# One select per attention item, with differences of two blocks' values, in a hybrid decoder block

## The chip, the cores and the metric

One core of a Trainium2 chip runs one decoder block on 2048 tokens. The metric is the device time of one execution in microseconds (us), the median of several runs. The engines are TensorE (PE, matmuls; PEld is its weight load), VectorE (DVE), ScalarE (ACT), GpSimd (POOL) and SyncE (SP, which issues the transfers). Each engine works through its own instructions in order and waits for the others by semaphores.

## The reference

The residual stream has 2048 tokens of 1024 numbers. What matters here is the first half of the block, cut to its core:

```python
h = rmsnorm(x, attn_norm)
z = h @ w_in            # -> [pool channels | q | k | v | gate_pool | gate_attn]
gates = sigmoid(z[gate part] + b_gate)
a = pool_mixer(u_pool, w_pool, pool_scale)      # causal means over 2, 4, 8, 16 tokens
q = partial_rope(rmsnorm(q, q_norm), positions) * scale
k = partial_rope(rmsnorm(k, k_norm), positions)
b = swa_sink_attention(q, k, v, sinks)          # 16 query heads, 2 key heads of 64
x = x + (g_pool * a + g_attn * b) @ w_out
# then rmsnorm, up-projection, causal convolution of 3, SiLU gate, down-projection
```

A query sees itself and the 127 tokens before it: in blocks of 128, the keys of its own block up to its own place, and the keys of the block before from the place after that. So each key place of 128 belongs to one of two blocks, and which one depends on whether it lies at or before the query's place.

## The kernel before, in words

The tokens are taken in two chunks (c = 0, 1) of 1024 tokens, or 8 blocks. All large matmuls are three products of high and low parts (`mm3`, L225 before and L235 after; the same weight tile, 8 steps of 3, makes a "fill" of 24 matmuls of 128x512). The parts are made by an ACT copy and a DVE subtraction (L209 and L210 for weights).

At the start, the head, the pool weights are folded (`fold`) while the first tokens and weights arrive; the tables of sines and cosines (`rope_tables`, L501 to L537) are made on DVE by one long chain of small operations. Then, in each chunk, a first stage makes keys and values block by block, with some fills between. Then comes attention: 32 items, in 4 groups of 4 heads (`q4` = 3, 2, 1, 0), each over 8 blocks. An item is

- scores: 8 matmuls into the one PSUM bank `s` (L770),
- on DVE: L779 copies the scores of the block before over the places that this query doesn't see in its own block (both blocks then share 128 key places), L784 takes the maximum, L785 and L786 scale and bound it; four exponentials on ACT (L791), and the normalisation (L795),
- transposes on PE into bank `t` (L802), the copy into high and low parts (ACT L804, DVE L805) as tile `M`,
- two selects on POOL (L808, L811), which separate the places of the own block from those of the block before,
- values: 4 matmuls into bank `a` (L824), copied out by L831 and L832 into `ob`, and multiplied with the gate by L834.

Between the items stand one or two fills each: projections of the attention gates (`ga`), the pool gates (`pg`), the pool channels (`pu`) and the queries (`q`). `fillers` and `first_fillers` deal them out to the places; `slabs_of(i)` are the two column slabs that belong to group i. Queries go to DRAM as high and low parts (`qd`) and come back item by item (`load_queries`), two items ahead. Small work behind a fill is collected in `later` and issued by `run_later`; the window sums of the pool channels are `windows` (L874, L885 and L886). The weights' order in SP's queue is `weight_order`: in the second chunk they are read back as ready parts (`made_...`). A scheduler with its own model of times then sets each engine's final order, so the code's order is only a wish. Tiles named `U`, `F`, `M`, `Q` and `R` are buffers of pools of 19, 4, 5, 5 and 3.

Of the kernel before, what the change touches and what calls it, by code (L numbers as in the profile page):

```python
# [121 lines left out]

def fillers(c, i):

    ga = [[("ga", ct, n) for n in range(2)] for ct in slabs_of(i + 1) if i < 3]
    pg = [[("pg", ct, n) for n in range(2)] for ct in slabs_of(i - 1) if i > 0]
    pu = [[("pu", ct, n) for n in range(2)] for ct in slabs_of(i)]
    fold = [[("fold", j, 0)] for j in FOLDS[FOLD_FIRST:] if c == 0 and i == 0]
    q = [queries_of(i)] if i < 2 else []
    out = sum(ga[:1] + pg[:1] + q + fold + pu[:1] + ga[1:] + pg[1:] + pu[1:], [])  # L130
    return [out[n * len(out) // NB:(n + 1) * len(out) // NB] for n in range(NB)]


def first_fillers(c):

    ga = [("ga", ct, n) for ct in slabs_of(0) for n in range(2)]
    q = queries_of(2) + queries_of(3)
    if c > 0:
        return [q[0:1], q[1:2], q[2:3], q[3:4], q[4:5], q[5:6], q[6:7], q[7:8] + ga]
    fold = [("fold", j, 0) for j in FOLDS[FOLD_LEAD:FOLD_FIRST]]  # L140
    return [[], fold[0:1], fold[1:2] + q[0:2], fold[2:3] + fold[3:4], q[2:4], q[4:5], q[5:6],
            q[6:8] + ga]


def weight_order():
    out = []
    for c in range(NCH):
        if c > 0:
            out.append(("kv",))
        else:  # L150
            out += [("fold", j) for j in FOLDS[:FOLD_LEAD]]
        out += [(kind, j) for parts in first_fillers(c) for kind, j, n in parts if n == 0]
        for i in range(4):
            out += [(kind, j) for parts in fillers(c, i) for kind, j, h in parts if h == 0]
        out += [("pg", ct) for ct in slabs_of(3)]
# [27 lines left out]
def block_kernel(ctx: ExitStack, tc: tile.TileContext, x, xT, pos, vec, qkn, w_poolT, w_pool, w_q, w_kv,  # L183
# [12 lines left out]
    qp = pool("qp", 5)  # L196
# [8 lines left out]
    def split(hi, lo, src):  # L205
        n = src.shape[1] // 2
        for i in range(2):
            t = slice(i * n, (i + 1) * n)
            A.copy(hi[:, t], src[:, t])  # L209
            V.tensor_sub(lo[:, t], src[:, t], hi[:, t].bitcast(F32))  # L210
# [49 lines left out]
    def split_weights(key, raws):  # L260
# [10 lines left out]
        for raw in raws:  # L271
            shape = [P, 2] + list(raw.shape)[1:]
            p, tag = (mp, "M") if out and key[1] not in FOLDS[:FOLD_LEAD] else (up_, "U")
            out.append(p.tile(shape, F32R, tag))
            hi, lo = out[-1][:, 0], out[-1][:, 1]
            split(hi, lo, raw)
# [84 lines left out]

    one = cp.tile([P, 1], F32, "one")
# [65 lines left out]
    for i in range(2):  # L428
# [4 lines left out]
    ones = qp.tile([P, P], F32, "Q")  # L433
    V.memset(ones, 1.0)
    identr = cp.tile([P, P], F32R, "identr")
    G.affine_select(identr, ones, pattern=[[-1, P]], base=0, channel_multiplier=1,
                    compare_op=ALU.is_equal, fill=0.0)
# [11 lines left out]
    hbg = cp.tile([P, 16], F32, "hbg")  # L449
    nsink = cp.tile([P, NH], F32, "nsink")  # L450
# [5 lines left out]
    def scaled():  # L456
        V.tensor_scalar(hbg, vc[:, V_BG:V_BG + 16], 0.5, None, op0=ALU.mult)
        V.tensor_scalar(nsink, vc[:, V_SK:V_SK + NH], -1.0, None, op0=ALU.mult)
# [6 lines left out]
    fix = cp.tile([P, 4, 16], F32, "fix")  # L465
    V.memset(fix, 1.0)
    for g, w in enumerate(WINDOWS):
        for t in range(w - 1):
            V.memset(fix[:, g, t:t + 1], w / (t + 1.0))
# [4 lines left out]
    kc = cp.tile([P, 2, 2, P], F32R, "kc")  # L474
    vcar = cp.tile([P, 2, P], F32R, "vcar")
# [20 lines left out]
    def rope_tables(chunk):  # L496

        n, at = [P, NB, 8], slice(chunk * NB, (chunk + 1) * NB)
        rt = mp.tile([P, 12, NB, 8], F32, "M")
# [126 lines left out]
    def rope(dst, src, b, nh):  # L626

        t = sp.tile([P, 2, nh, 16], F32, "rope", 1)
# [20 lines left out]
    def keys_values(c, hs, ws):  # L649
        kts = [up_.tile([P, 2, T], F32R, "U") for _ in range(2)]  # L650
        vs = up_.tile([P, NB, 2, P], F32R, "U")
# [10 lines left out]
        def block_a(n, pk):  # L662
# [3 lines left out]
            A.activation(vs[:, n, :, 0:HD], pv, AF.Copy, scale=rn)  # L666
            V.scalar_tensor_tensor(vs[:, n, :, HD:P], pv, rn, vs[:, n, :, 0:HD].bitcast(F32),
                                   op0=ALU.mult, op1=ALU.subtract)
            r = head_rstd(pk, 2, c, n)
            kq = kns[n] = qp.tile([P, 2, 80], F32, "Q")  # L670
            kn = kq[:, :, 0:HD]
            V.tensor_tensor(kn, pk[:, 0:128].rearrange("p (g d) -> p g d", g=2),
# [3 lines left out]
        def block_b(n):  # L676
            c_, kq = slice(n * P, (n + 1) * P), kns.pop(n)
            kn, kr = kq[:, :, 0:HD], kq[:, :, HD:80]
            rope(kr, kn, c * NB + n, 2)
# [15 lines left out]
        return kts, vs, raw, block_a, block_b, turn  # L695
# [9 lines left out]
    def queries(c, j, n, hs, ta, st):  # L705
        if n == 0:
            st["q", j] = stream.get("q", j, later=later)
        pq, c_ = project(hs, st["q", j], n, "fa"[j % 2])
        sq = qp.tile([P, 512], F32, "Q")
        A.square(sq, pq)  # L710
        if j % 2 == 0:
            st["even"] = pq, sq
            return
        pe, acc = st.pop("even")
# [4 lines left out]
        for i, src in ((at - 1, pe), (at, pq)):  # L719
            t = mp.tile([P, 2, 512], F32R, "M")  # L720
            A.copy(t[:, 0], src)
            V.tensor_sub(t[:, 1], src, t[:, 0].bitcast(F32))
            for e, r in enumerate(STARTS[i]):
                load(qd[own][n][:, r:r + 8].rearrange("a d h t -> (d h) a t"),
                     t[64 * e:64 * e + 64].bitcast(F32))
# [12 lines left out]
    def rotate(a, b, rows, c_):  # L738
# [3 lines left out]
        ga, gb = (vc[h, V_QG + i:V_QG + i + 1] for i in range(2))  # L742
        t = mp.tile([P, 2, 512], F32, "M")
        for i, (x, g) in enumerate(((a, ga), (b, gb))):
            V.scalar_tensor_tensor(t[h, i], x[h], g, s, op0=ALU.mult, op1=ALU.mult)
            V.scalar_tensor_tensor(x[h], x[h], g, c, op0=ALU.mult, op1=ALU.mult)
        V.tensor_sub(a[h], a[h], t[h, 1])
        V.tensor_add(b[h], b[h], t[h, 0])

    def load_queries(it):  # L750
# [5 lines left out]
        it["rq"] = rq[:, q4 // 2, n, h:h + 4]  # L756

    def scores(it):
# [6 lines left out]
        for h in range(4):  # L765
# [7 lines left out]
            if n == 0 and b > 0:  # L773
                for a in range(2):
                    nc.tensor.matmul(sc[:, h, 0:P], st, kc[:, g, a, :], start=(a == 0),
# [22 lines left out]
    def probabilities(it):  # L798
        b = it["c"] * NB + it["n"]
        pp = ps.tile([P, 4, P], F32, "t")  # L800
        for h in range(4):
# [4 lines left out]
        pin = pa.bitcast(F32).rearrange("p a h q -> p (a h) q")  # L806
        cur = mp.tile([P, 2, 4, P], F32R, "M")
        G.affine_select(cur.rearrange("p a h q -> p (a h) q"), pin, pattern=[[0, 8], [1, P]],  # L808
                        base=0, channel_multiplier=-1, compare_op=ALU.is_ge, fill=0.0)
        if b > 0:  # L810
            G.affine_select(pa.rearrange("p a h q -> p (a h) q"), pin, pattern=[[0, 8], [-1, P]],  # L811
                            base=0, channel_multiplier=1, compare_op=ALU.is_gt, fill=0.0)
        it.update(cur=cur, prev=pa)

    def values(it):
        c, n, g, vs = it["c"], it["n"], it["q4"] // 2, it["vs"]
        todo = [(vs[:, n, g, :], it["cur"])]
        if c * NB + n > 0:
            todo.append((vs[:, n - 1, g, :] if n > 0 else vcar[:, g, :], it["prev"]))
# [8 lines left out]
        pe = pv.rearrange("p (c e) q -> p e c q", e=2)  # L828
        for e in range(2):
# [4 lines left out]
        V.scalar_tensor_tensor(tt, tt, 1.0, ob, op0=ALU.add, op1=ALU.mult)  # L834
# [12 lines left out]
    def gate_attn(c, ct, n, hs, ta, st):  # L847
        if n == 0:
            st["ga", ct] = stream.get("ga", ct, later=later)
            if ct % 2 == 0:  # L850
                ta[ct // 2] = up_.tile([P, 2, T], F32, "U")
        pg, c_ = project(hs, st["ga", ct], n)
        V.tensor_mul(pg, pg, rB[:, c_])
        A.activation(ta[ct // 2][:, ct % 2, c_], pg, AF.Tanh, scale=0.5, bias=hbg[:, 8 + ct:9 + ct])
# [12 lines left out]
    def windows(c, ct, u, st):  # L867
        g, win = ct // 2, WINDOWS[ct // 2]
# [14 lines left out]
        def finish():  # L883
            if c == 0:
                V.tensor_mul(s[:, 16:32], s[:, 16:32], fix[:, g, :])  # L885
# [460 lines left out]
    def mixer(c, hs, kvw):  # L1346
# [38 lines left out]
        for i in range(len(items)):  # L1385
            group, n = divmod(i, NB)
            scores(items[i])
            if i + 2 < len(items):
                load_queries(items[i + 2])
            fills = fillers(c, group)[n]  # L1390
            if i > 0 and len(fills) == 1:
                probabilities(items[i - 1])
            run_later()
# [7 lines left out]
        for n in range(2):  # L1401
            gated(c, slabs_of(3)[0], n, hs, ta, st)
        values(items[-1])
        run_later(9)
        if c + 1 < NCH:
            for g in range(2):
                A.copy(kc[:, g], kts[g][:, :, T - P:T].bitcast(F32))
            A.copy(vcar, vs[:, NB - 1].bitcast(F32))
        ms = [mixed(ta, j) for j in (3, 2, 1)]
        for n in range(2):  # L1410
            gated(c, slabs_of(3)[1], n, hs, ta, st)
# [3 lines left out]
    scaled()  # L1415
# [86 lines left out]
```

## Time and profile before

| | us |
|---|---|
| runs | 2477.36, 2484.81, 2481.82 (median 2481.82) |
| profiled execution | 2475.48, span 2473.8 |
| PE busy | 2416.9 (98%) |
| DVE busy | 1901.9 (77%) |
| ACT busy | 1101.3 (45%) |
| POOL busy | 226.5 (9%) |
| L808, 64 selects | 84.7, 1323 ns each |

The profile comes from one execution; its own time is 2475.48 us. In rows of the trace "x24" is a count, "a<-M,U" names what is written and read, and a bracket at the end says how long the engine stood idle before and who released it. The attention of the first chunk lies at about 142 to 530 us, that of the second at 1356 to 1745 us.

### The profile page before, as it was taken

How to read it: one execution, taken by the hardware profiler on the slowest of the kernel's cores; microseconds unless marked ns; L12 is line 12 of the kernel's file. 1: busy time of each engine (PE TensorE's matmuls, PEld its weight loads, DVE VectorE, ACT ScalarE, POOL GpSimd, SP SyncE). 2: the span in 40 equal slices, each digit the busy share in tenths (PEclk: the TensorE clock that was granted, in tenths of full speed). 3: DMA queues.
4: the chain of work that ended last, by engine and by line, in shares of the span. 5: the costliest groups of instructions: out<-in, count | busy, mean ns of one | idle time of the engine just before them, and what ended most of it. 6: DMA issues, size and time to landing. Idle time of an engine off the chain costs nothing.

```text
span 2473.8 us, 30606 instructions
## 1 busy us (share of the span) xinstructions
PE 2416.9 (98%) x11360; PEld 2003.3 (81%) x11360; DVE 1901.9 (77%) x3047; ACT 1101.3 (45%) x2106; POOL 226.5 (9%) x161
## 2 busy tenths in 40 slices
PE   7999999899999999999999999999999999999999
PEld 6887887777888888888888888777888888887887
DVE  7668778977887887899844666678569888788994
ACT  6443444445455555543512333334435555454432
POOL 0112322310000000000002113213000000000000
PEclk9999999999999999999999999999999999999999
DMA  9662725248332233544343432320553222228321
GB/s 338 231 214 84 243 98 177 75 167 275 128 103 77 85 115 116 179 179 162 109 163 120 137 128 86 141 94 22 168 190 102 78 78 93 86 68 281 127 78 51
DMA packets 137620, 336.68 MB, mean 136 GB/s; under 512 B 12160, under 2 KB 47232, under 8 KB 126464
## 3 DMA queue, kind: packets, MB, share of 16 engines
q1 hardware_dynamic: 137472, 334.74, 39.7%
q8 instruction: 89, 1.46, 0.2%
q14 instruction: 59, 0.48, 0.1%
HBM read 230.88 MB, written 103.81 MB: 135 GB/s over the span
## 4 chain that ended last, share of the span: by engine, by line
PE 80%; DVE 12%; ACT 3%; DMA 2%; issue 2%; POOL 1%; SPq 0%; DVEq 0%; ACTq 0%; POOLq 0%
PE f L225 22%; PE f L1037 18%; PE t L1037 9%; PE a L225 4%; PE a L1037 4%; PE a L1327 4%; PE f L1327 4%; PE s L1327 4%; PE t L1327 4%; PE s L770 1%; ACT Q L791 1%; DVE F L874 1%; DVE U L210 1%; PE a L824 1%; DVE Q L832 1%
## 5 line engine op out<-in xcount | busy, mean ns | idle before, releaser
L225 PE MATMUL f<-U,U 128*128 128x512 f32 (+1 forms) x3552 | 832.6, 390 | 16.3 <-DVE U L210 7.6
L225 PEld LDWEIGHTS f<-U,U 128*128 128x128 f32 x3552 | 654.6, 189 | 151.0 <-DVE U L210 11.4
L1037 PE MATMUL f<-U,U 128*128 128x512 f32 x1512 | 359.7, 389 | 1.3 <-ACT Q L1055 1.3
L1037 PEld LDWEIGHTS f<-U,U 128*128 128x128 f32 x1512 | 283.3, 188 | 61.5 <-ACT Q L1055 2.2
L1103 DVE SCALAR_TENSOR_TENSOR M<-F,vc,M 128x1024 f32<-128x1024 f32 x176 | 224.9, 1281 | 128.2 <-ACT M L1100 127.8
L1037 PE MATMUL t<-U,U 128*128 128x512 f32 x1080 | 254.2, 389 | 0.0
L1037 PEld LDWEIGHTS t<-U,U 128*128 128x128 f32 x1080 | 202.7, 188 | 42.1
L791 ACT ACTIVATE Q<-s,st,rq 128x128 f32<-128x128 f32 x256 | 114.2, 452 | 157.9 <-DVE st L786 145.6
L321 ACT CAST U<-R 128x1024 fp32r<-128x1024 f32 x120 | 125.5, 1053 | 65.6 <-DVE R L342 33.9
L322 DVE TENSOR_TENSOR U<-R,U 128x1024 fp32r<-128x1024 f32 x120 | 146.6, 1221 | 0.1
L225 PE MATMUL a<-U,U 128*128 128x256 f32 (+1 forms) x768 | 142.3, 339 | 2.1 <-DVE M L510 1.3
L1037 PE MATMUL a<-U,U 128*128 128x512 f32 x576 | 138.6, 389 | 0.0
L808 POOL TENSOR_SCALAR_AFFINE_SELECT M<-M 128x1024 fp32r<-128x1024 f32 x64 | 84.7, 1323 | 569.7 <-DVE M L805 391.6
L225 PEld LDWEIGHTS a<-U,U 128*128 128x128 f32 x768 | 119.5, 189 | 17.7 <-ACT rB L570 1.5
L1037 PE MATMUL f<-U,M 128*128 128x512 f32 x504 | 122.3, 390 | 4.1 <-DVE F L1081 4.1
L1037 PEld LDWEIGHTS a<-U,U 128*128 128x128 f32 x576 | 108.0, 188 | 22.3
L1286 ACT CAST U<-U 128x1024 fp32r<-128x1024 f32 x74 | 77.0, 1050 | 86.9 <-PE a L1327 26.9
L1037 PEld LDWEIGHTS f<-U,M 128*128 128x128 f32 x504 | 94.4, 188 | 24.4 <-DVE F L1081 4.9
L210 DVE TENSOR_TENSOR U<-R,U 128x512 fp32r<-128x512 f32 x142 | 97.8, 721 | 17.3 <-ACT U L209 17.2
L1100 ACT ACTIVATE M<-F,vc 128x1024 f32<-128x1024 f32 x88 | 109.2, 1243 | 1.3
L1089 ACT COPY F<-f 128x512 f32<-128x512 f32 x42 | 24.6, 586 | 178.7 <-PE f L1037 178.7
L1287 DVE TENSOR_TENSOR U<-U,U 128x1024 fp32r<-128x1024 f32 x74 | 89.5, 1218 | 10.6 <-ACT U L1286 10.6
(270 smaller groups left out, 3754.2 us busy)
## 6 DMA issues: line engine op xcount, KB each, us to landing
R<-w_up SPq DMA_DIRECT2D x80, 512.0 KB, 3.7
actd<-M SPq DMA_DIRECT2D x44, 512.0 KB, 2.6
U<-w_down SPq DMA_DIRECT2D x88, 256.0 KB, 5.2
U<-actd SPq DMA_DIRECT2D x88, 256.0 KB, 5.3
qd<-M SPq DMA_DIRECT2D x64, 256.0 KB, 3.4
Q<-qd SPq DMA_DIRECT2D x64, 256.0 KB, 3.0
R<-w_out SPq DMA_DIRECT2D x32, 512.0 KB, 5.1
U<-kept SPq DMA_DIRECT2D x12, 1024.0 KB, 6.5
```

The costliest lines, as they stand in the source:

```text
L210: V.tensor_sub(lo[:, t], src[:, t], hi[:, t].bitcast(F32))
L225: nc.tensor.matmul(out, a, b, start=(i == 0), stop=(i == n - 1))
L321: A.copy(t[:, 0], raw)
L322: V.tensor_sub(t[:, 1], raw, t[:, 0].bitcast(F32))
L791: A.activation(pr[:, h, :], sc[:, h, 0:P], AF.Exp, bias=nm[:, h:h + 1], scale=it["rq"][:, h:h + 1], accum_out=rs[:, h:h + 1])
L808: G.affine_select(cur.rearrange("p a h q -> p (a h) q"), pin, pattern=[[0, 8], [1, P]], base=0, channel_multiplier=-1, compare_op=ALU.is_g ...
L1037: nc.tensor.matmul(bank, a[:, x, k, :], b[k // 2][:, y, k % 2, :], start=(first and i == 0), stop=(i == 11), skip_group_check=True)
L1100: A.activation(y, u[:, 2:], AF.Identity, bias=cw[:, 3, m:m + 1], scale=cw[:, 2, m:m + 1])
L1103: V.scalar_tensor_tensor(y, u[:, j:j + T], cw[:, j, m:m + 1], y, op0=ALU.mult, op1=ALU.add)
L1286: A.copy(hi, src)
L1287: V.tensor_sub(lo, src, hi.bitcast(F32))
L1327: nc.tensor.matmul(into[m], u[:, 0, c_], v[:, 1], start=(first and j == 0), stop=(k == n - 1 and j == 2), skip_group_check=True)
```

## The change

1. Instead of separating both blocks' places by two selects, one select keeps the own block's places (`own`), and the unselected tile stands for all places (`all`). The values are then the values of the block before times `all`, plus the difference of the two blocks' values, `vd`, times `own`. `vd` is made in the first stage, with its own high and low parts.
2. `values` of an item is called two items later, behind that item's scores, in place of one item later at the item's end.
3. The two gates' projections of a slab run together, one group later; all queries of the first half run in group 0. The groups of the second chunk get 10, 12, 12 and 12 fills in place of 12, 16, 12 and 8, and the end of attention 8 in place of 4. The attention gate goes into a tile of its own and is multiplied in `later`; `ob` is written straight into `ta`.
4. Queries are copied raw from PSUM to SBUF by ACT; rotation and splitting read that copy.
5. In the head: the identity is built first, 38 matmuls on it that nobody reads (`idle`) come first on PE, and the scaling of constants is issued behind the first split of weights.
6. The last block's keys and values pass to the second chunk by DRAM (`carry`).

```diff
+def gates_of(i):
+    return [(kind, ct, n) for ct in slabs_of(i) for kind in ("ga", "pg") for n in range(2)]
 def fillers(c, i):
-    ga = [[("ga", ct, n) for n in range(2)] for ct in slabs_of(i + 1) if i < 3]
-    pg = [[("pg", ct, n) for n in range(2)] for ct in slabs_of(i - 1) if i > 0]
-    pu = [[("pu", ct, n) for n in range(2)] for ct in slabs_of(i)]
-    fold = [[("fold", j, 0)] for j in FOLDS[FOLD_FIRST:] if c == 0 and i == 0]
-    q = [queries_of(i)] if i < 2 else []
-    out = sum(ga[:1] + pg[:1] + q + fold + pu[:1] + ga[1:] + pg[1:] + pu[1:], [])
+    g = gates_of(i - 1) if i > 0 else queries_of(0) + queries_of(1)
+    pu = pooled_of(i)
+    if i == 0:
+        pu = pu[2:]
+    fold = [("fold", j, 0) for j in FOLDS[FOLD_FIRST:] if c == 0 and i == 0]
+    out = fold + g[:4] + pu[:2] + g[4:] + pu[2:]
     return [out[n * len(out) // NB:(n + 1) * len(out) // NB] for n in range(NB)]
...
-    qp = pool("qp", 5)
+    qp = pool("qp", 6)
...
+    idle = ps2.tile([P, T], F32, "s")
+    for _ in range(38):
+        nc.tensor.matmul(idle[:, 0:512], identr, identr.unsqueeze(1).to_broadcast([P, 4, P]),
+                         start=True, stop=True)
...
     def block_a(n, pk):
...
+            if c * NB + n > 0:
+                d = q[:, :, 80:80 + HD]
+                V.tensor_sub(d, v, vf[:, (n - 1) % 2])
+                A.copy(vd[:, n, :, 0:HD], d)
+                V.tensor_sub(vd[:, n, :, HD:P], d, vd[:, n, :, 0:HD].bitcast(F32))
...
     def queries(c, j, n, hs, ta, st):
...
-        pq, c_ = project(hs, st["q", j], n, "fa"[j % 2])
+        pq, c_ = project(hs, st["q", j], n)
+        if j % 2 == 0:
+            st["raw"] = mp.tile([P, 2, 512], F32, "M"), qp.tile([P, 512], F32, "Q")
+        raw, acc = st["raw"]
+        A.copy(raw[:, j % 2], pq)
...
+        parts = up_.tile([P, 2, 2, 512], F32R, "U")
         if j % 4 == 1:
-            rotate(pe, pq, st["rows"], c_)
+            rotate(raw, st["rows"], c_, parts[:, 0].bitcast(F32))
+        A.copy(parts[:, 0], raw)
+        V.tensor_sub(parts[:, 1], raw, parts[:, 0].bitcast(F32))
...
     def probabilities(it):
...
-        if b > 0:
-            G.affine_select(pa.rearrange("p a h q -> p (a h) q"), pin, pattern=[[0, 8], [-1, P]],
-                            base=0, channel_multiplier=1, compare_op=ALU.is_gt, fill=0.0)
-        it.update(cur=cur, prev=pa)
+        it.update(all=pa, own=own)
...
     def values(it):
...
+            todo = [(vs[:, n - 1, g, :] if n > 0 else it["carry"][:, 2], it["all"]),
+                    (vd[:, n, g, :], it["own"])]
...
-            V.tensor_add(ob[own], pe[own, e], ob[own])
-        tt = it["ta"][it["q4"]][:, :, n * P:(n + 1) * P]
-        V.scalar_tensor_tensor(tt, tt, 1.0, ob, op0=ALU.add, op1=ALU.mult)
+            V.tensor_add(tt[own], pe[own, e], ob[own])
...
     def gate_attn(c, ct, n, hs, ta, st):
...
-        A.activation(ta[ct // 2][:, ct % 2, c_], pg, AF.Tanh, scale=0.5, bias=hbg[:, 8 + ct:9 + ct])
+        A.activation(t, pg, AF.Tanh, scale=0.5, bias=hbg[:, 8 + ct:9 + ct])
+        later.append(lambda: V.scalar_tensor_tensor(x, t, 1.0, x, op0=ALU.add, op1=ALU.mult))
...
             scores(items[i])
             if i + 2 < len(items):
                 load_queries(items[i + 2])
+            if i > 1:
+                values(items[i - 2])
+            run_later()
             fills = fillers(c, group)[n]
...
-            if i > 0:
-                values(items[i - 1])
...
-    scaled()
+    with tc.issue_after(split_weights.last):
+        scaled()
     rope_tables(0)
```

How the order of instructions moves at the places that matter, as the scheduler leaves it (a number behind a letter tells one buffer from another).

PE, second chunk, third group, a place with one fill. Before:

```order
L225 MATMUL f_13481<-U_10345,U_13439 128x512 x3
L824 MATMUL a_13508<-M_13477,U_10406 128x512 x2
L824 MATMUL a_13508<-M_13474,U_10406 128x512 x2
L770 MATMUL s_13519<-U_10404,Q_13356 128x256 x8
L802 MATMUL t_13545<-identr_136,Q_13429 128x128 x4
L225 MATMUL f_13560<-U_10200,U_13439 128x512 x3
```

After, in the same group:

```order
L235 MATMUL f_12985<-U_10364,U_12863 128x512 x3
L797 MATMUL s_13012<-U_10423,Q_12851 128x256 x8
L854 MATMUL a_13038<-M_12980,U_10425 128x512 x2
L854 MATMUL a_13038<-M_12983,U_10426 128x512 x2
L829 MATMUL t_13078<-identr_91,Q_12949 128x128 x4
L854 MATMUL a_13140<-M_13083,U_10425 128x512
L235 MATMUL f_13052<-U_10219,U_12971 128x512 x3
```

The values matmuls moved from ahead of the next scores to behind them, and one of the next item's (it reads `M_13083`, made of bank `t_13078`) stands right behind its own transposes.

DVE, the same group, from the scores of an item to the bound of the maximum. Before:

```order
L832 TENSOR_TENSOR Q_13407<-a_13402,Q_13407 64x256
L779 COPY_PREDICATED s_13413<-causal_142,s_13413 128x4x128
L832 TENSOR_TENSOR Q_13407<-a_13402,Q_13407 64x256
L784 TENSOR_REDUCE st_13423<-s_13413 128x4
L834 SCALAR_TENSOR_TENSOR U_12089<-U_12089,Q_13407 128x2x128
L785 SCALAR_TENSOR_TENSOR st_13423<-st_13423,rq_193 128x4
L786 TENSOR_TENSOR st_13423<-st_13423,nsink_147 128x4
```

After, at an item with window work and a one-fill item:

```order
L906 TENSOR_TENSOR F_13152<-F_13050 128x1038
L806 COPY_PREDICATED s_13114<-causal_181,s_13114 128x4x128
L906 TENSOR_TENSOR F_13153<-F_13152 128x1036
L811 TENSOR_REDUCE st_13124<-s_13114 128x4
L832 TENSOR_TENSOR M_13161<-t_13156,M_13161 128x512
L812 SCALAR_TENSOR_TENSOR st_13124<-st_13124,rq_229 128x4
L918 SCALAR_TENSOR_TENSOR F_13153<-F_13153,F_13050 128x1024
L813 TENSOR_TENSOR st_13124<-st_13124,vc_145 128x4
```

The gate's multiplication L834 is gone from between; at this item the window sums and the subtraction of the transposed tile stand in its place.

ACT at the start of the program. Before:

```order
L365 ACT_TABLE_LOAD
L365 ACTIVATE first_91<-one_89 128x1
L209 CAST U_124<-R_93 128x512 x2
L209 CAST U_129<-F_97 128x256 x2
L209 CAST U_282<-R_94 128x512 x2
```

After:

```order
L385 ACT_TABLE_LOAD
L385 ACTIVATE first_134<-one_132 128x1
L551 ACTIVATE ck_219<-F_237 128x8x8 x2
L218 CAST U_167<-R_136 128x512 x2
L218 CAST U_172<-F_140 128x256 x2
L218 CAST U_318<-R_137 128x512 x2
```

The sines of the first rope table (`ck`), which need the whole chain on DVE, moved ahead of the first high parts of the weights.

More of the change, by code (lines that the diff above doesn't have):

```diff
@@ L275, in split_weights @@
             hi, lo = out[-1][:, 0], out[-1][:, 1]
-            split(hi, lo, raw)
+            split_weights.last = split(hi, lo, raw)
         return out if len(out) > 1 else out[0]
@@ L694, in turn @@
                 V.tensor_copy(kts[g][:, :, c_], pt[:, g].bitcast(F32))
-        return kts, vs, raw, block_a, block_b, turn
+        return kts, (vs, vd), raw, block_a, block_b, turn
     qd = [[dp.tile([2, HD, 8, 512], F32, f"qd_{i}_{n}") for n in range(2)] for i in range(2)]
@@ L756, in load_queries @@
         it["rq"] = rq[:, q4 // 2, n, h:h + 4]
+        if c > 0 and n == 0:
+            it["carry"] = qp.tile([P, 3, P], F32R, "Q")
+            load(it["carry"].bitcast(F32), carry[q4 // 2])
     def scores(it):
@@ L1397, in mixer @@
                 filler(*f, c, hs, ta, st)
-            if i > 0:
-                values(items[i - 1])
+        values(items[-2])
+        run_later()
         between.append(lambda: probabilities(items[-1]))
-        for n in range(2):
-            gated(c, slabs_of(3)[0], n, hs, ta, st)
+        rest = gates_of(3)
+        for f in rest[:2]:
+            filler(*f, c, hs, ta, st)
         values(items[-1])
```

134 lines of the change are left out of this document (69 added, 65 removed).

## Prediction

> **What bounds the kernel now.** I read the page's busy shares first, then the chain of waits of TensorE over the two attention stretches (142 to 530 us, 1356 to 1745 us), then busy time by attention group, then the timeline of single items.
>
> ```profile
> PE 2416.9 (98%) x11360; PEld 2003.3 (81%) x11360; DVE 1901.9 (77%) x3047; ACT 1101.3 (45%) x2106; POOL 226.5 (9%) x161
> ...
> 142.00:231.00 89.00, 85.80 (x430) 71.42 (x429) 69.22 (x143) 39.01 (x118) 17.31 (x13) 1.00 0.45 154
> ...
> 341.00:430.00 89.00, 85.68 (x417) 70.22 (x416) 73.80 (x149) 41.78 (x124) 21.12 (x15) 1.00 0.52 184
> 430.00:507.00 77.00, 70.31 (x349) 57.16 (x348) 71.69 (x140) 39.14 (x114) 22.23 (x15) 1.00 0.20 62
> 1356.00:1445.00 89.00, 87.25 (x438) 72.81 (x438) 61.45 (x126) 32.18 (x104) 17.68 (x14) 1.00 0.31 104
> 1445.00:1554.00 109.00, 108.86 (x537) 91.34 (x536) 67.06 (x136) 35.59 (x112) 29.38 (x18) 1.00 0.34 116
> 1554.00:1645.00 91.00, 86.44 (x427) 71.61 (x426) 61.50 (x126) 31.21 (x104) 19.13 (x16) 1.00 0.35 128
> 1645.00:1720.00 75.00, 69.61 (x344) 55.68 (x342) 65.70 (x127) 35.87 (x108) 20.69 (x16) 1.00 0.15 50
> sum 729.00, PE 702.49 PEld 580.09 DVE 549.56 ACT 298.60 POOL 177.74; mean PE 87.81 PEld 72.51 DVE 68.69 ACT 37.32 POOL 22.22
> ```
>
> TensorE (PE) is the bound, busy 98%. Only its idle time can be won, and the windows of the four groups of each chunk (columns: length, then busy us of PE, PEld, DVE, ACT, POOL) show where a large part lies: 729.00 − 702.49 = 26.5 us idle in attention. The second group, with two fills behind every item, loses 0.14 us in the second chunk (its row for the first chunk is left out, the sum holds it); the fourth groups, with one fill, lose 6.7 and 5.4, and there DVE is busy 71.69 of 77. The waits of PE, first chunk and then second:
>
> ```profile
> PE a L824 <- POOL M L811: 6.7, 10, 1.4
> PE s L770 <- ACT Q L791: 3.1, 3, 1.7
> PE a L824 <- POOL M L808: 2.6, 5, 0.9
> ...
> PE s L770 <- ACT Q L791: 6.6, 7, 1.5
> PE a L824 <- POOL M L811: 2.1, 6, 0.4
> PE a L824 <- POOL M L808: 1.5, 2, 1.0
> ```
>
> Two waits alternate. The values matmuls wait for the selects (23 times, 6.7 + 2.6 + 2.1 + 1.5 = 12.9 us); the scores wait for their single PSUM bank, which the last exponential frees (10 times, 9.7 us). An undisturbed item's start and the next one's, and an item with a bank wait, give their true size:
>
> ```profile
> 1459.19 1.12 PE L770 MATMUL s<-U,Q 128*128 128x256 f32 x8
> ...
> 1472.46 0.75 PE L770 MATMUL s<-U,Q 128*128 128x256 f32 x5
> ...
> 1699.49 1.12 PE L770 MATMUL s<-U,Q 128*128 128x256 f32 x8
> 1700.48 0.66 PE L802 MATMUL t<-identr,Q 128*128 128x128 f32 x4
> 1700.89 5.71 PE L225 MATMUL f<-U,U 128*128 128x512 f32 x24
> 1706.44 1.07 PE L824 MATMUL a<-M,U 128*128 128x512 f32 x4
> 1708.28 1.22 PE L770 MATMUL s<-U,Q 128*128 128x256 f32 x8 [0.77 <-ACT Q L791]
> ```
>
> An undisturbed item with two fills takes 1472.46 − 1459.19 = 13.27 us. A fill is 1706.44 − 1700.89 = 5.55, so a one-fill item should take 7.72. This one took 1708.28 − 1699.49 = 8.79: 1.07 lost where 0.77 is shown, since a matmul's end hides the first part of a stop. About 0.3 more is lost at each wait. With the 33 waits of the rows above attention really loses about 26.5 + 33 × 0.3 = 36.4 us. That is all that the attention edits can win.
>
> **The change part by part.**
>
> *One select less per item, and values two items later.* The select wait is made of a chain: transposes, ACT copy, DVE subtract, first select, second select. Both go here:
>
> ```profile
> 1602.07 0.60 PE L802 MATMUL t<-identr,Q 128*128 128x128 f32 x4
> 1602.78 0.59 ACT L804 CAST M<-t 128x512 fp32r<-128x512 f32 x1 [1.10 <-PE t L802]
> ...
> 1604.16 1.09 POOL L808 TENSOR_SCALAR_AFFINE_SELECT M<-M 128x1024 fp32r<-128x1024 f32 x1 [5.05 <-DVE M L805]
> 1605.32 1.36 POOL L811 TENSOR_SCALAR_AFFINE_SELECT M<-M 128x1024 fp32r<-128x1024 f32 x1
> 1605.64 1.05 DVE L785 SCALAR_TENSOR_TENSOR st<-st,rq 128x4 f32<-128x4 f32 x1
> ...
> L785 DVE SCALAR_TENSOR_TENSOR st<-st,rq x64: 144/155/1050, 145.7 to 1713.0; 128x4 f32<-128x4 f32 x64
> ```
>
> The second select's end moves up by 1.36 here; and in the order the values stand behind the next scores, one group of eight matmuls (1700.48 − 1699.49 = 1 us) further from their transposes. So "two items later" in the code is 1 us more cover in the order, 2.4 with the select. The longest select wait shown is 1.4. The select waits go: 23 × (12.9 / 23 + 0.3) = 19.8 us. What is late next is the score bank: PE arrives there earlier.
>
> *Gates one group later.* The second chunk's groups hold 12, 16, 12, 8 fills before and 10, 12, 12, 12 after; two fills leave the first stage and two the groups, four go behind the last group, and the total stays the same, so the work itself costs 0. One-fill turns rise from 4 + 0 + 4 + 8 = 16 to 6 + 4 + 4 + 4 = 18 per chunk, 12 of them in the last three groups: 24 in both chunks. Each is a place for a bank wait. In the turn above the bank is asked for 1708.28 − 0.77 = 1707.51 and is 0.77 late; of its chain one 0.42 us operation goes (the gate's L834, which stands between the maximum and its scale), and where a select ran against L785 (1.05 instead of 0.155) 0.9 goes too in the turns that had the second select beside them. Against it, window operations of 1.23 us stand in the chain of some turns after. Bounds per turn: 0, if both gains hold, and 0.94 + 0.3 = 1.24, the mean of the second chunk's seven. I take 0.45, nearest to 0.77 − 0.42 = 0.35 plus something for the windows: 24 × 0.45 = 10.8 us.
>
> *A values matmul that stands too early.* In the second chunk one values matmul stands directly behind its own item's transposes, three times. It needs only the ACT copy, which ends 1603.37 − 1602.67 = 0.7 after the transposes above, more where other ACT work goes first; the far bound is the end of the first select, 1605.25 − 1602.67 = 2.6. I take 1.5, between them: 4.5 us.
>
> *First group.* The queries move into it and it has 10 instead of 12 fills. It loses 3.2 + 1.75 = 5 now. Bounds: 5, as now, and 5.4 + 5.4 = 10.8, if both become what the second chunk's last group is; I take 8. The queries' own price, and the first stage that holds the rest of them:
>
> ```profile
> L721 ACT CAST M<-f x16: 576/587/626, 65.9 to 1494.5; 128x512 fp32r<-128x512 f32 x16
> ...
> L834 DVE SCALAR_TENSOR_TENSOR U<-U,Q x64: 415/425/1309, 165.5 to 1732.5; 128x256 f32<-128x256 f32 x64
> ...
> 52.00:142.00 90.00, 89.15 (x489) 76.69 (x489) 50.20 (x146) 31.75 (x72) 15.75 (x8) 1.00 0.68 237
> ```
>
> 32 more raw copies by ACT at 0.587 = 18.8 us on an engine busy 45%: PE's fills hide it. L834 goes 64 times (0.425 each, 27 us) and 32 operations of twice its size come, at most 2 × 0.425 each, 27 us: no change. The first stage also gets the differences of values, two small operations each on DVE and ACT per block; PE idles 90 − 89.15 = 0.85 us there and DVE is busy 56%, so they cost 0; without that cover 15 × 4 operations of up to 0.425 would show 26 us.
>
> *The rule that speaks against the raw queries.* The trace shows DVE held for 1.05 where it needs 0.155, right behind a select's start. The Trainium skill, "SBUF — State Buffer", section "Who interferes with whom", says that a DVE operation with two SBUF inputs contends with a GpSimd one that reads SBUF, and that the loser blocks fully. L785 (both inputs in SBUF) agrees. By this rule the rotation, which now reads its queries from SBUF instead of PSUM, becomes exposed in the first group: by it the sum would rise by at most 16 selects × 1.09 = 17 us of DVE time, of which DVE's idle there hides most; by the trace's one direct row it stays in the 8.
>
> *Other edits.* The last block's keys and values go to the second chunk through DRAM, by four stores and four small loads, the loads two items ahead; the DMA engines are busy 0.31 in that window, so 0 while a load lands within an item (7.72 us). The smaller tables and the sixth Q buffer cost nothing.
>
> *The head.* The rope table's chain now stands ahead of the first subtractions on DVE, and its two sines ahead of ACT's first casts.
>
> ```profile
> 0.79 0.39 SPq L203 DMA_DIRECT2D posi<-pos  x1
> ...
> 4.95 1.14 ACT L209 CAST U<-R 128x512 fp32r<-128x512 f32 x2 [2.67 <-DMA R<-w_poolT]
> ...
> 16.58 1.09 PE L225 MATMUL f<-U,U 128*128 128x256 f32 x7 [1.21 <-ACT F L610]
> ...
> 572.58 0.17 DVE L501 CAST M<-posi 128x8 f32<-128x8 int32 x1
> 580.67 0.18 DVE L536 TENSOR_SCALAR M<-M 128x64 f32<-128x64 f32 x1
> ...
> 16.60:34.50 17.90, 16.60 (x136) 16.27 (x136) 16.04 (x66) 16.78 (x40) 1.97 (x2) 1.00 0.96 353
> ```
>
> The chain alone took 580.67 + 0.18 − 572.58 = 8.3 us. It needs the positions, issued first, at 0.79 + 0.39, and there by 4.95, when a larger load behind them is; so it ends between 9.5 and 13.2. I take 11: ACT's casts start 6 us later than 4.95. But ACT's waits of 2.67 and more for weights then lie behind it: it catches up to within 1 to 3 us when the second fold starts at 16.58. In return 8.3 us leave DVE between 16.6 and 52, where the DMA engines are busy 0.96 and set the pace. The 38 idle matmuls on the new identity, at 5.55 / 24 = 0.23 each 8.8 us from the start on, end by then and cost 0, or 1 to 2 if they run slower. I take +1, bounds −3 (chain gone from a busy stretch) and +5 (all of the delay).
>
> **Sum.** Attention 10.8 + 4.5 + 8 = 23.3 instead of 36.4: −13.1; head +1; −12.1. From the profiled 2475.48 (1.7 of it around the span of 2473.8, unchanged) that is 2463.4. The median of the three runs shown is 6.3 above the profiled one, so on its scale 2481.8 − 12.1 = 2469.7.
>
> **The rivals.**
> 1. *The bank wait takes the place of the select wait.* For it: the second chunk already loses more to the bank (6.6) than to the selects (3.6), and DVE is busy 93% in the last group. Each of 24 turns pays 1.24: 29.8 + 4.5 + 8 = 42.3 against 36.4, +5.9, with the head 2488.7. From 0.65 a turn on, 24 × 0.65 + 12.5 + 1 = 29 against 36.4, the gain is within 7.4, and from 0.95 on there is none. Against it: fewer locks and no L834 in the chain.
> 2. *More gain.* Bank waits vanish with the locks, early matmuls wait 0.7, the first group stays at 5: 3 × 0.7 + 5 = 7 instead of 36.4, head −1: 2451. Against it: a turn with windows in its chain.
> 3. *Slower: weight loads late in the second chunk.* Four of its 1 MB loads now stand behind query loads in SP's queue, which wait for a free buffer.
>
> ```profile
> 1602.26 9.37 SPq L203 DMA_DIRECT2D Q<-qd  x2
> ...
> U<-made_ga SPq DMA_DIRECT2D x8, 1024.0 KB, 7.8
> ```
>
> If such a hold of 9.37 falls before a load that takes 7.8, and the order leaves a fill and two items' other matmuls (13.27 − 2 × 5.55 = 2.17 each) for both, 9.9, each is 7.3 late: 4 × 7.3 = 29, giving 2499. It decides above (12.1 + 7.4) / 4 = 4.9 each. Against it: by the order the buffer comes free with the scores of two items before, so that the hold need not fall ahead of these loads.
> 4. *The change does not do what it says*: the values move by 1 us only, and a select wait can stay where ACT is late. It is inside rival 1's sum.
>
> **How the numbers follow.** No change is what lies within 0.3% (7.4 us), about what a measurement of this kernel tells apart. Forecast 0.62 (its own range 2460 to 2481: head −3 with turns of 0.2, and head +5 with turns of 0.75), rival 1 with 4: 0.18, more gain 0.11, slower 0.09. Faster is more gain plus some six in seven of the forecast, 0.11 + 0.54 = 0.65; same is rival 1 and the forecast's upper end, 0.18 + 0.08 = 0.26; slower 0.09. The range reaches from near the gain's 2451 to near rival 1's 2489: 2452 to 2487.
>
> **What would show it.** Right: no values wait on a select in the list of PE's waits, or under 3 us; bank waits near 24 × 0.15 shown; three waits of values on ACT in the second chunk; first real matmul at 11.5 to 13 us and the second fold by 20; POOL near 150 us. Wrong: bank waits above 20 us shown; PE waiting for a DMA in the second chunk; a second fold later than 22 us.

## The result, and the profile after

The changed kernel takes 2462.8 us (median; 2459.19 to 2464.95), the kernel before 2480.48 (2474.89 to 2484.81) in the same series. The ratio is 0.993, with an interval of 0.9911 to 0.9948: 17.7 us faster. The forecast was 2469.7, 12.1 faster, in a range of 2452 to 2487. The profiled execution took 2459.19 us, its span is 2456.9, 16.9 less than before.

The first line of the page (busy time by engine) and the list of what PE waited for (total, times, longest) of the changed kernel:

```profile
PE 2421.4 (99%) x11398; PEld 2010.8 (82%) x11398; DVE 1876.9 (76%) x3028; ACT 1124.8 (46%) x2150; POOL 146.5 (6%) x101
...
PE s L797 <- ACT Q L818: 9.7, 16, 1.8
...
PE f L235 <- ACT F L624: 3.2, 1, 3.2
PE t L753 <- DVE Q L740: 2.6, 4, 1.0
PE a L854 <- ACT M L831: 2.2, 3, 0.7
PE a L235 <- DVE Q L694: 1.5, 2, 1.0
```

No values matmul (L854) waits for POOL any more; before, 23 did. The scores (L797) wait for their bank 16 times instead of 10, for the same 9.7 us. The three waits of L854 for the ACT copy are the values matmuls that stand directly behind their own transposes. DVE does 25 us less, POOL 80. Busy time by attention group, four of each chunk, in windows that begin at the groups' first scores:

```profile
131.00:210.00 79.00, 76.03 (x385) 61.76 (x384) 67.03 (x135) 40.44 (x117) 15.94 (x8) 1.00 0.52 167
210.00:297.00 87.00, 85.67 (x428) 71.77 (x427) 64.92 (x138) 41.27 (x121) 15.50 (x9) 1.00 0.50 175
297.00:383.00 86.00, 84.47 (x417) 70.19 (x416) 66.47 (x139) 38.27 (x116) 10.04 (x8) 1.00 0.39 135
383.00:462.00 79.00, 78.29 (x389) 65.30 (x388) 63.53 (x133) 39.61 (x117) 9.19 (x7) 1.00 0.41 146
1333.00:1413.00 80.00, 76.47 (x390) 62.59 (x389) 61.33 (x122) 34.91 (x108) 13.97 (x8) 1.00 0.44 140
1413.00:1503.00 90.00, 88.02 (x433) 73.67 (x432) 57.08 (x120) 33.79 (x107) 15.07 (x9) 0.98 0.32 111
1503.00:1590.00 87.00, 85.81 (x427) 71.84 (x426) 58.89 (x121) 31.66 (x104) 10.46 (x8) 1.00 0.28 100
1590.00:1672.00 82.00, 80.38 (x401) 67.06 (x400) 54.97 (x117) 32.09 (x104) 8.57 (x7) 1.00 0.31 106
sum 670.00, PE 655.14 PEld 544.17 DVE 494.23 ACT 292.04 POOL 98.75; mean PE 81.89 PEld 68.02 DVE 61.78 ACT 36.51 POOL 12.34
```

PE is idle 670.00 − 655.14 = 14.9 us in attention, instead of 26.5. The last groups lose 0.7 and 1.6 us instead of 6.7 and 5.4; DVE is busy 63.53 of 79 there. The first groups now lose the most, 3.0 and 3.5. The head, from PE's and ACT's timeline:

```profile
1.47 11.77 PE L380 MATMUL s<-identr 128*128 128x512 f32 x38 [1.47 <-POOL identr L375]
10.90 1.13 ACT L218 CAST U<-R 128x512 fp32r<-128x512 f32 x2
13.07 3.17 PE L235 MATMUL f<-U,U 128*128 128x256 f32 x24
19.43 1.82 PE L235 MATMUL f<-U,U 128*128 128x256 f32 x13 [3.19 <-ACT F L624]
```

The 38 idle matmuls run until the first real ones at 13.07; those then take 3.17 us for 24, where before 22 took 4.24. The kernel before, at the same place:

```profile
11.13 4.24 PE L225 MATMUL f<-U,U 128*128 128x256 f32 x22 [3.63 <-DVE U L210]
```

The second fold starts at 19.43 instead of 16.58.

### The profile page after: what moved, and what is told of

It reads as the page before. It is cut to its first block, busy times and chain, and to the rows that moved or that the text cites. A ratio compares the mean times of both kernels' runs of the same rounds, so it can differ in the third digit from the quotient of the medians.

```text
span 2456.9 us, 30720 instructions
## 1 busy us (share of the span) xinstructions
PE 2421.4 (99%) x11398; PEld 2010.8 (82%) x11398; DVE 1876.9 (76%) x3028; ACT 1124.8 (46%) x2150; POOL 146.5 (6%) x101
## 4 chain that ended last, share of the span: by engine, by line
PE 87%; DVE 8%; ACT 2%; DMA 1%; issue 1%; POOL 0%; SPq 0%; DVEq 0%; ACTq 0%; POOLq 0%
PE f L235 31%; PE f L1069 18%; PE t L1069 10%; PE a L1069 4%; PE a L1359 4%; PE f L1359 4%; PE s L1359 4%; PE t L1359 4%; PE s L797 2%; PE a L854 2%; PE a L235 2%; DVE F L906 1%; ACT Q L818 1%; PE t L829 1%; PE t L753 1%
## 5 line engine op out<-in xcount | busy, mean ns | idle before, releaser
L235 PE MATMUL f<-U,U 128*128 128x512 f32 (+1 forms) x3936 | 918.8, 389 | 7.9 <-DVE U L219 3.7
L235 PEld LDWEIGHTS f<-U,U 128*128 128x128 f32 x3936 | 725.4, 188 | 158.3 <-DVE U L219 7.2
L1069 PEld LDWEIGHTS f<-U,U 128*128 128x128 f32 x1512 | 283.3, 188 | 61.6 <-ACT Q L1087 2.2
L1069 PEld LDWEIGHTS a<-U,U 128*128 128x128 f32 x576 | 108.0, 188 | 22.3
L1069 PEld LDWEIGHTS f<-U,M 128*128 128x128 f32 x504 | 94.4, 188 | 24.4 <-DVE F L1113 4.9
L218 ACT CAST U<-R 128x512 fp32r<-128x512 f32 x142 | 80.6, 617 | 20.4 <-DMA R<-w_ga 5.1
L1318 ACT CAST F<-U 128x1024 fp32r<-128x1024 f32 x46 | 48.3, 1050 | 88.2 <-PE a L1359 52.3
```

What stands on the lines that cost most here:

```text
L235: nc.tensor.matmul(out, a, b, start=(i == 0), stop=(i == n - 1))
L1069: nc.tensor.matmul(bank, a[:, x, k, :], b[k // 2][:, y, k % 2, :], start=(first and i == 0), stop=(i == 11), skip_group_check=True)
L1318: A.copy(hi, src)
```

## The experiments

Each run is a kernel of its own, timed against the kernel before on the same chip (medians of before: 2479.1 to 2479.4). An interval is that of the ratio to the kernel before. The changed kernel was timed once, in its own series (2480.48 for the kernel before), so a difference in us between it and a run below also holds the 1.1 to 1.4 us by which the series differ. A profile shows one execution, which need not be the one of the median.

**Two selects again.** In the changed kernel both selects return, the differences go.

```diff
+        if b > 0:
+            G.affine_select(pa.rearrange("p a h q -> p (a h) q"), pin, pattern=[[0, 8], [-1, P]],
+                            base=0, channel_multiplier=1, compare_op=ALU.is_gt, fill=0.0)
...
+        todo = [(vs[:, n, g, :], it["own"])]
         if c * NB + n > 0:
-            todo = [(vs[:, n - 1, g, :] if n > 0 else it["carry"][:, 2], it["all"]),
-                    (vd[:, n, g, :], it["own"])]
-        else:
-            todo = [(vs[:, n, g, :], it["own"])]
+            todo.append((vs[:, n - 1, g, :] if n > 0 else it["carry"][:, 2], it["all"]))
```

> The changed kernel, with both selects again and without the differences of values. Theory (the select wait is what the change removes): a second select ends 1.1 to 1.4 us later behind the first, and its place one group of scores later gives back 1 us, so waits of the values for POOL return, 3 to 7 us in the chain of waits where the changed kernel has none, and the bank waits grow by up to 5 us by DVE held beside POOL: 2467 to 2475 us. Rival (the new deal of the fills did it): no waits on POOL, time within 3 us of 2462.8.

2476.37 us, ratio 0.9993 (0.9984 to 1.0002): 13.6 of the gain are gone, a little more than the range allowed. Page line and waits:

```profile
PE 2431.8 (98%) x11398; PEld 2013.4 (81%) x11398; DVE 1901.3 (77%) x2998; ACT 1122.9 (45%) x2135; POOL 223.0 (9%) x161
...
PE s L792 <- ACT Q L813: 14.4, 20, 2.0
...
PE a L850 <- POOL M L835: 2.4, 6, 0.6
```

Little of that is waits for POOL, 2.4 us. DVE is busy 24.4 us longer, with fewer instructions, and the bank waits are 4.7 longer. I added up, over the trace, how much longer than the median of their line and shape DVE's operations are where they overlap a select (only those over by 0.15 us): 49.8 us in 67 operations here, 20.9 in 29 in the changed kernel, 50.2 in 63 in the kernel before. In these three traces no DVE operation is that much over its median unless it overlaps a select.

**Values one item later.** In the changed kernel the values are called at the item's end again, ahead of the next scores.

```diff
-            if i > 1:
-                values(items[i - 2])
...
+            if i > 0:
+                values(items[i - 1])
```

> The changed kernel, with the values one item later, ahead of the next scores, as before the change. Theory: 1 us of cover goes, one select alone is 1.4 us earlier than two, so waits on POOL of up to 4 us shown and no more bank waits: 2463 to 2469 us. Rival (the place of the values is the main part): waits of 12 us on POOL, 2475 us or more.

2462.14 us, 0.9933 (0.992 to 0.9946): no difference. Its list has two short waits of values for POOL. With one select the place of the values is worth nothing that can be seen here.

```profile
PE s L797 <- ACT Q L818: 10.0, 16, 1.5
...
PE a L854 <- POOL M L835: 0.6, 2, 0.4
```

**Both undone.**

> The changed kernel with both undone: two selects, values one item later. Theory: the select waits of before (12.9 us shown, 20 with what a stop costs more) return at 24 instead of about 20 one-fill turns; head and deal of the fills are as changed: 2477 to 2487 us. Rival (the deal of the fills did it): 2463 to 2468 us.

2492.93 us, 1.0056 (1.004 to 1.0071), 13.5 slower than the kernel before and above my theory's range:

```profile
PE s L792 <- ACT Q L813: 16.4, 26, 2.1
PE a L850 <- POOL M L835: 7.7, 14, 1.4
...
PE a L850 <- POOL M L831: 2.2, 5, 0.7
```

So the two parts overlap and don't add up. With two selects the later values are worth 2492.9 − 2476.4 = 16.5 us, with one nothing. The one select is worth 2492.9 − 2462.1 = 30.8 with the values one item later, and still 13.6 with the values two items later: it makes the later place needless, but not the other way round.

**The gates one group later alone**, put into the kernel before (new `fillers`, `gates_of`, the gate's product in `later`).

> The kernel before with the gates one group later alone (new deal of fills, the gate's product behind the values). Theory: waits are spread over more one-fill turns, not removed: select waits as before or up to 5 us more, 2478 to 2488 us. Rival (the deal did it): the last groups lose 3 us less each, 2463 to 2470 us.

2492.56 us, 1.0055 (1.0042 to 1.0069): 13 us slower. Its waits:

```profile
PE s L779 <- ACT Q L800: 13.1, 22, 2.1
...
PE a L833 <- POOL M L820: 7.9, 13, 1.3
PE a L833 <- POOL M L817: 6.7, 8, 3.4
```

Both kinds grow: the select waits from 12.9 to 14.6 us, which is within the 5 us I allowed, and the bank waits, which I had left out, from 9.7 to 13.1. With 43 waits instead of 33 and about 0.3 more for each, that is some 8 of the 13 us; the rest isn't traced. Alone in the kernel before, this part of the change is a loss, not a gain.

**Two more half selects per item**, behind the one select, on a tile that was already read (`pr`).

```diff
+        pr = it["pr"].rearrange("p h q -> p (h q)")
+        for _ in range(2):
+            G.affine_select(pr, pr, pattern=[[0, 4], [1, P]], base=0, channel_multiplier=-1,
+                            compare_op=ALU.is_ge, fill=0.0)
```

> The changed kernel with two more selects of half the size per item on POOL, behind the one select, on a buffer that nobody reads any more: POOL works as much as before the change, but no values matmul waits for it. Theory L (what the second select cost was DVE held beside POOL, which shows as waits for the score bank): DVE busy grows by about 24 us to 1900, bank waits from 9.7 to about 14 us shown, 2468 to 2476 us. Rival C (its place in the chain to the values): DVE the same, bank waits the same, within 3 us of 2462.8.

2477.2 us, 0.9989 (0.9981 to 0.9998): 14.4 slower than the changed kernel, as much as with the second select and above the range, though no matmul needs its result.

```profile
PE 2426.8 (98%) x11398; PEld 2014.7 (82%) x11398; DVE 1901.9 (77%) x3028; ACT 1125.8 (46%) x2150; POOL 251.0 (10%) x229
...
PE s L797 <- ACT Q L818: 15.1, 18, 1.9
...
L841 POOL TENSOR_SCALAR_AFFINE_SELECT Q<-Q 128x512 f32<-128x512 f32 x128 | 104.0, 813 | 443.0 <-PE t L829 354.5 <-ACT Q L868 44.5 <-DVE s L806 16.3
```

DVE is busy 1901.9, as with two selects; bank waits 15.1. But it isn't quite the same load: the half selects keep POOL busy for 104.0 us, where the 60 selects that came back above took 75.9.

**Zeros in place of the half selects**, the same tile, the same place.

```diff
-            G.affine_select(pr, pr, pattern=[[0, 4], [1, P]], base=0, channel_multiplier=-1,
-                            compare_op=ALU.is_ge, fill=0.0)
+            G.memset(pr, 0.0)
```

> As the run with two more half selects per item, but POOL fills the same dead buffer with zeros instead: POOL is busy and the buffer is held about as long, and nothing is read from SBUF. Theory (DVE is held by a POOL operation that reads SBUF, as the Trainium skill has it in 'SBUF — State Buffer', 'Who interferes with whom'): DVE excess beside POOL and time as in the changed kernel, 2460 to 2466 us. Rival 1 (the buffer held longer was the cost) or rival 2 (any POOL work holds DVE): 2471 us or more.

2469.84 us, 0.9958 (0.9946 to 0.9971), between both theories; the interval just touches that of the changed kernel and is clear of that of the half selects.

```profile
PE 2431.1 (98%) x11398; PEld 2016.5 (82%) x11398; DVE 1890.3 (77%) x3028; ACT 1125.4 (46%) x2150; POOL 213.9 (9%) x229
...
PE s L797 <- ACT Q L818: 11.1, 18, 1.9
...
L841 POOL MEMSET Q<- 128x512 f32 x128 | 67.3, 526 | 454.0 <-PE t L829 370.0 <-ACT Q L867 34.8 <-DVE s L806 21.2
```

No DVE operation that overlaps only a fill with zeros is more than 0.1 us over its median. The Trainium skill's rule ("SBUF — State Buffer", "Who interferes with whom": contention with a GpSimd operation that reads SBUF, not with one that only writes it) agrees with that. Beside the half selects that read, 34 operations are over by more than that, 10.3 us in all. But in both runs DVE also loses 34 us beside the one real select, not 20.9: its two small operations on the maximum (L813, L814) meet it more often. DVE's order is the same in the three kernels, so this is a shift in time; what makes it, the tile held longer or something else, no run separates. Of the 14.4 us, about 7.4 are what the half selects cost beyond the fills (2477.2 − 2469.8), by reading or, in part, by being longer (813 ns instead of 526). The other 7 come with the fills too; that this shift causes them is likely, but not shown.

**Queries from PSUM**, as before the change, the two of a pair in banks f and a.

```diff
-        pq, c_ = project(hs, st["q", j], n)
...
-        A.copy(raw[:, j % 2], pq)
...
+        pq, c_ = project(hs, st["q", j], n, "fa"[j % 2])
...
```

> The changed kernel with the queries rotated and split from PSUM as before, the two of a pair in banks f and a. Theory of the prediction (the raw copies are hidden and cost 0): within 3 us of 2462.8, and the first groups lose the same 6 us. Rival (rotation out of SBUF is held by POOL, or the fills wait less for a bank with raw copies): first groups lose 3 us each more or less.

2470.66 us, 0.9969 (0.9958 to 0.9979), 7.9 slower, where my theory said within 3. In its first group, windows and PE's timeline:

```profile
154.00:161.00 7.00, 4.30 (x16) 2.29 (x14) 5.33 (x12) 3.39 (x11) 1.09 (x1) 0.87 0.49 134
161.00:168.00 7.00, 5.27 (x16) 4.07 (x17) 5.55 (x13) 4.96 (x12) 0.00 (x0) 0.50 0.25 80
...
156.81 0.47 PE L852 MATMUL a<-M,U 128*128 128x512 f32 x1 [0.61 <-DVE M L744]
157.92 0.50 PE L852 MATMUL a<-M,U 128*128 128x512 f32 x1 [0.64 <-DVE M L830]
159.08 1.12 PE L852 MATMUL a<-M,U 128*128 128x512 f32 x2 [0.66 <-DVE st L810]
161.28 2.07 PE L795 MATMUL s<-U,Q 128*128 128x256 f32 x8 [1.09 <-ACT Q L816]
```

L744 is the subtraction that splits a query from PSUM. Three stops of 0.6 to 0.7 us stand close together. Then the granted clock (the third number from the end of a window's row) falls to 0.50, at about 159.2 us by the 0.87 of the first window, and the eight score matmuls take 2.07 us instead of 1.12. The second chunk's first group shows much the same. Each of the two stretches at half clock is 10.2 us long, which costs up to 5.1 us, so most of the 7.9 us can be the clock and not the stops themselves. So the raw copies are a part of the gain in their own right, with this deal of the fills.

**The old deal of the fills** in the changed kernel (12, 16, 12, 8, the gate ahead of the values).

> The changed kernel with the fills dealt out as before (12, 16, 12, 8; attention gate ahead of the values and its product at the item). Theory (the deal alone made the kernel before 13 us slower, since it makes more one-fill turns): with one select those turns cost little, so a small gain from fewer of them against two window operations more per turn of the last group: 2456 to 2464 us. Rival (one select needs the new deal): the last group loses 6 us each chunk again, 2470 us or more.

2459.11 us, 0.9924 (0.991 to 0.9938); 3.7 faster, within the intervals of both. Bank waits 13.9 us, half of it (6.9) in the last groups, none of values for POOL, and one wait for a weight load:

```profile
PE s L788 <- ACT Q L809: 13.9, 16, 1.7
...
PE f L226 <- DMA U<-made_ga: 1.5, 1, 1.5
```

**The old head** in the changed kernel.

> The changed kernel with the head as before (no idle matmuls, identity later, scaling of constants first, rope table in M). Theory of the prediction: head cost +1, bounds -3 and +5, so this one is 1 us faster, 2459 to 2466 us; first fold matmuls again slow, 22 in 4.2 us. Rival (the head is part of the gain): slower by 3 us or more, 2466 us up.

2459.07 us, 0.9919 (0.9906 to 0.9932); 3.7 faster, and again the intervals overlap. The first folds are as before, slow at first:

```profile
6.64 0.80 PE L235 MATMUL f<-U,U 128*128 128x256 f32 x2 [6.64 <-ACT U L218]
11.02 4.87 PE L235 MATMUL f<-U,U 128*128 128x256 f32 x22 [3.59 <-DVE U L219]
16.43 3.16 PE L235 MATMUL f<-U,U 128*128 128x256 f32 x24 [0.54 <-ACT F L619]
```

The second fold starts 3.0 us earlier than in the changed kernel.

**The score bank in two halves**, two heads each, released one by one.

```diff
-        sc = ps2.tile([P, 4, 256], F32, "s")
+        scs = [ps2.tile([P, 2, 256], F32, t) for t in ("s", "s2")]
...
```

> The changed kernel with the scores of two heads each in a PSUM bank of their own, released one by one, and the copy over the mask and the maximum as two DVE operations each. Theory (what is left in attention is the score bank): scores start two exponentials, 1.3 us, earlier, bank waits of 9.7 us go to under 3 us shown, 12 us less with what a stop costs more; against it 4 more small DVE operations per item: 2450 to 2458 us. Rival (DVE, not the bank, is the limit): the same or slower, 2460 to 2470 us.

2460.42 us, 0.9923 (0.9909 to 0.9936): 2.4 faster by the medians, within the intervals and in the rival's range. The bank waits do shrink, to 3 of 3.7 us in all, but the time gains less than they did:

```profile
PE s L803 <- ACT Q L826: 3.7, 3, 3.1
```

**Together:** the old deal with the old head, then with the split bank.

> The changed kernel with both the old deal of the fills and the old head. If the two gains of 3.7 us add: 2455 us. If they were one and the same drift of the machine: 2459 us.

2458.37 us, 0.9919 (0.9905 to 0.9932): the two don't add up to 7.4, and 2459 is what I had expected if neither is a gain of its own.

> The same with the scores' bank in two halves. Bank waits of 13.9 us (old deal) go below 4 us shown: 2447 to 2453 us if DVE has room in the last group; 2455 us if not.

2450.55 us, 0.9886 (0.9873 to 0.99): 12 us faster than the changed kernel, its interval clear of that one's, and the fastest version here.

```profile
PE s L789 <- ACT Q L812: 6.1, 12, 1.0
```

The bank waits go from 13.9 to 6.1 us, about as much less as in the changed kernel (9.7 to 3.7), where the time hardly moved.

The granted clock is a part of these last comparisons. The result of every run gives its mean granted clock. Over the 77 runs of the twelve kernels above, each set against the mean of its own kernel, 0.001 less clock goes with about 2.0 us more time. The means are 0.9970 for the changed kernel, 0.9983 with the old deal, 0.9955 with the split bank, 0.9995 with old deal, old head and split bank, and 0.9944 with queries from PSUM. By this estimate 5.2 of the 7.9 us of the queries from PSUM are clock, 2.6 of the old deal's 3.7 us are, the split bank alone loses 3 us to it, and of the 12 us of the fastest version 5 are clock. Whether an order of instructions brings its clock about or met it by chance, these runs don't separate. The two selects (0.9969) had the same clock as the changed kernel, so their 13.6 us aren't touched.

## Why the prediction was right, point by point

- *The select wait goes* (19.8 us with what a stop costs more): right, none is left. The reason was only half right. I put it down to the chain to the values. But when the second select came back, the time rose by 13.6 us with only 2.4 us of waits for POOL, and two half selects that nobody waits for cost 14.4. In both runs DVE is held longer beside POOL, which the prediction had only as a bonus for some turns of the score bank. How much of the price that holding is stays open: of the 14.4 us, 7.4 go with what the half selects do beyond a fill, and the rest comes with the fills too, which themselves hold nothing.
- *Two items later is 1 us more cover*: with one select it is worth nothing, with two 16.5 us. The prediction added up the cover of the two parts, where the one select alone is enough.
- *Bank waits of later groups*, 24 × 0.45 = 10.8: the list shows 16 in all, and 8 of these, 5.5 us, are in the windows of the first groups. 9.7 − 5.5 + 8 × 0.3 = 6.6. The term was too high, and made of other parts: 8 turns of 24 wait, and each loses about 0.8, not 0.45. The 0.45 also starts from a wait as shown (0.77 − 0.42) and leaves out the 0.3 that its own upper bound has. That fewer turns wait because POOL holds DVE less is likely, but not shown.
- *The early values matmul*, 3 × 1.5: three waits, 2.2 + 3 × 0.3 = 3.1, each near the lower bound of 0.7.
- *First groups*, 8: 2.97 + 3.53 idle, plus 0.3 for each of ten waits, 9.5. Close, but its price for the raw queries was wrong: I took 0 and a rule that speaks against them. Without them the kernel loses 7.9 us, by the estimate above mostly (5.2) through the granted clock. What I missed: without raw copies DVE works on the queries in PSUM, in a bank that the values need next; one wait of 0.61 us for L744 shows that, and the clock behind such stops is the larger cost.
- *The deal of the fills costs 0*: alone it costs 13 us; in the changed kernel undoing it gave 3.7 by the medians, within the intervals and mostly clock by the estimate above. The prediction's price for its turns was too low without the one select.
- *Head*, +1, up to +5: first real matmul at 13.07 (11.5 to 13 was said) and second fold at 19.43 (by 20). The old head is 3.7 faster by the medians, within the intervals.
- *Late weight loads* in the second chunk (rival 3): no wait of PE for a transfer there. Rival 1, the bank in place of the selects, is what two selects with later values show: 14.4 us of bank waits and nearly the time of before.
- *The sum*: attention was to keep 23.3; it keeps 14.9 + about 23 × 0.3 = 22. The result is 5.6 us better than the forecast. One suspect is the granted clock between 575 and 590 us, first of the kernel before, then of the changed one:

```profile
575.00:590.00 15.00, 14.27 (x63) 11.54 (x62) 10.31 (x39) 6.10 (x12) 1.39 (x1) 0.89 0.90 296
...
575.00:590.00 15.00, 14.98 (x70) 11.99 (x68) 9.11 (x12) 6.72 (x11) 0.00 (x0) 1.00 0.61 217
```

But the changed kernel has a drop of the same length in attention (the 0.98 in its row of 1413 to 1503), so this is not what parts the two executions. To see what does, I counted each matmul at the median distance of its shape from start to start in the trace before (0.227 us for 128x512, 0.120 for 128x256) and the idle matmuls of the head at nothing, and took the rest of each stage as lost. Up to attention 20.9 us become 20.3, in the two stretches of attention 42.3 become 28.1, between them 11.9 become 10.1 and behind them 12.1 become 11.8: 16.9 less in all. So attention gave 14.2 where 13.1 was forecast, the start gave 0.6 where it was to cost 1, and the rest gave 2.1 where nothing was forecast; why, stays open.

That the number came so close is luck in part. The sum counts what is left in attention, not what each part of the change takes away, so it could come out right while the price of the select had half its cause and the raw queries, worth 7.9 us, had none.

## What to carry to other kernels

Before you price an instruction on GpSimd by who waits for its result, see how long VectorE's operations beside it become; here a select's return cost 13.6 us, and the list of waits showed 2.4 of it as waits for GpSimd. Parts of a change that shorten the same wait don't add up: undo them one by one and together. And look at which parts only pay with others. Here the gain came from the one select and the raw queries; the later place of the values adds nothing to the one select, and the new deal of the fills and the new head could not be told from no gain. Read the granted clock of the runs before you explain a difference of a few us.

## What the runs showed of the hardware

- A fill with zeros on POOL (526 ns in the mean, 128 times) made no VectorE operation more than 0.1 us longer than its median; a select on the same tile (813 ns in the mean) did so to 34 operations, by 10.3 us in all.
- In the run with queries from PSUM three stops of PE of 0.6 to 0.7 us within 3 us were followed by 10.2 us of a granted clock of 0.50, with matmuls at half pace. From 154 to 175 us PE was idle for 4.4 us, but by the count of matmuls used above 9.3 us were lost: this cluster of small stops cost about twice what the idle time shows.
